# Kept inputs of a convolution: four 24-row turns become one 128-row turn

## The chip, the cores and the metric

One core of a Trainium2 chip runs one program. The metric is the device time of one execution in microseconds (us), as the median over runs. The engines are named as the profile names them: PE is TensorE (PEld its weight loads), DVE is VectorE, ACT is ScalarE, POOL is GpSimd, and SP is the engine on whose queue almost all transfers (DMAs) are issued.

## The reference, cut to what matters

Two decoder layers run over a prompt of 1024 tokens and over 8 samples of 4 tokens each. Layer 0 is sliding-window attention. Layer 1 is gated DeltaNet, and the change is in it. Its input projection gives q, k, v, z and two gates; q, k and v (4096 channels in all) pass a causal convolution of 4 taps over time, channel by channel:

```python
xqkv, z, a, b = jnp.split(h @ w_in, [GDN_CONV_CH, ...], axis=-1)
xpad = jnp.concatenate([conv_buf.astype(xqkv.dtype), xqkv], axis=1)
conv = lax.conv_general_dilated(xpad, conv_w[:, None, :], ..., feature_group_count=GDN_CONV_CH)
conv = jax.nn.silu(conv)
q, k, v = jnp.split(conv, [GDN_K_W, 2 * GDN_K_W], axis=-1)
```

For the prompt `conv_buf` is zero. For the samples it is the input `state_gdn_conv`: the 3 last inputs of each of the 8 samples, 24 rows of 4096 channels. These are the "kept inputs". A chunked delta rule over 16 value heads (8 query/key heads) follows, then a norm, a gate by z and an output projection. New conv and delta-rule states are outputs too.

## The kernel before

The activations stand transposed, with channels on the 128 partitions and the 1056 tokens (1024 of the prompt, then 32 of the samples) along the free axis. The projection of layer 1 goes in channel tiles of 128: `project` multiplies a tile's weights with all tokens in three groups of 512, 256 and 288 tokens, and each group is 24 matmuls (8 slices of the model width, times three products of high and low float32r halves: wh and wl of the weights, h2hi and h2lo of the activations) into a PSUM bank `ps_pj`. There are two such banks.

The list `SEQ` gives the order of the tiles. A head group (`hq`, 8 of them) has a k tile, a q tile and two v tiles; 16 z tiles stand between. `conv(ct, ...)` projects one of the 32 tiles that are convolved. Its `evac` copies each group from the bank to `XR` on ACT (two buffers of XR), does tap 0 on ACT, and weaves in the job `taps`, which does taps 1 to 3 on DVE and a SiLU on ACT. With the third group, which holds the samples, it fetches the tile's 24 kept rows into `st` (24 x 128, one buffer) and weaves in the job `samples`. That one turns `st` on PE (`ps_tr<-cst,st`), turns 128 columns of XR (`ps_tr<-cst,XR`), copies the kept inputs to `XS` and the new conv state to `cvo` on ACT, sends `cvo` out, and does the samples' taps on POOL.

All other work of the layer is woven between the projection's matmuls as jobs too: `decay_blocks` masks the tiles `DP` on DVE and takes their exponentials on ACT; `solve` and `invert` invert 32 x 32 blocks on DVE (`X` and `tmp`, 31 steps of two instructions per head group), send them through DRAM (`Xdd`, `Xc`) and spread them on POOL (`Xd`); `blocks` builds the inverse `UZ` on PE; `chain` runs the recurrence chunk by chunk (`vo`, `us`, `uo`, `S`); `gating` turns the result for the output projection.

The order is planned while the program is built. `Core` records each instruction and keeps a modelled time per engine; a job goes on when `ready`, `soon`, `idle` or `bank` says so by that model. `K` gives each job's rank, and `LATE` holds single steps back, by job name, how often that job has been woven, and step:

```python
if eng in self.last:
    self.tc.add_manual_dep(ins, self.last[eng], ..., reason="program order")
...
d = LATE.get((e[2], e[4], e[5]))
...
return nc.free["tensor"] < e[6] + d
```

The compute engines run in the order that was recorded. Transfers on SP are not tied to it. Since every instruction goes through one wrapper, the profile names line 90 for nearly all of them; they are told apart by the names of the tiles.

Of the kernel before, what the change touches and what calls it, by code (L numbers as in the profile page):

```python
# [5 lines left out]
F32 = mybir.dt.float32  # L6
# [8 lines left out]
P = 128  # L15
D = 1024
KD = D // P
TP = 1024
# [10 lines left out]
HQ = 8  # L29
# [197 lines left out]
def body(tc, I, O, cst_ap, dbg=None):  # L227
    nc = tc.nc
# [12 lines left out]
    turns = dict.fromkeys(rings, 0)  # L241
# [11 lines left out]
    XE = ('vector', 'vector', 'vector', 'vector', 'vector', 'scalar', 'vector', 'scalar', 'vector')  # L253
    EV = [('vector', 'scalar')] * 9
    SX = ('vector',) * 8
    K = dict(turns=4, evac=3, squares=2, scales=1, rows=0, mods=5, shapes=6, weights=7, loads=8, low=5, split=3, add=3, attend=12, turning=14, modulate=31, cached=9, wo=7, turn=0, ahead=6, taps=4, gating=5, decay=2, samples=28, load=5, mod=9, shape=9, decays=8, prepare=1, gather=11, finish=54, states=21, core=4, new=9)
    KR = [{'chain': 8, 'output': 9, 'solve': 5, 'invert': 21, 'blocks': 10, 'decayed': 0}, {'chain': 0, 'output': 3, 'solve': 12, 'invert': 10, 'blocks': 35, 'decayed': 35}, {'chain': 33, 'output': 2, 'solve': 22, 'invert': 19, 'blocks': 33, 'decayed': 34}, {'chain': 22, 'output': 12, 'solve': 3, 'invert': 4, 'blocks': 30, 'decayed': 17}, {'chain': 14, 'output': 0, 'solve': 1, 'invert': 17, 'blocks': 31, 'decayed': 57}, {'chain': 3, 'output': 13, 'solve': 6, 'invert': 20, 'blocks': 55, 'decayed': 29}, {'chain': 8, 'output': 1, 'solve': 11, 'invert': 20, 'blocks': 73, 'decayed': 34}, {'chain': 10, 'output': 8, 'solve': 4, 'invert': 28, 'blocks': 40, 'decayed': 44}]
    TB = (3, 6)
    SW = (1, 16)
# [14 lines left out]
    def psb(tag=None):  # L274
        tag = tag or any_bank
        if tag in rings:
            turns[tag] += 1
            tag = rings[tag][(turns[tag] - 1) % len(rings[tag])]
        t = ps.tile([P, 512], F32, tag=tag, name="ps_" + tag, bufs=banks[tag])
        return nc.slot(tag, banks[tag], t) if isinstance(nc, Core) else t  # L280
# [11 lines left out]
    nc = Core(tc)  # L292
# [31 lines left out]
    ident = C["ident"]  # L324
# [3 lines left out]
    rows = xp.tile([64, P], F32, name="rows")  # L328
# [190 lines left out]
    def weave(gen, name, hq=None):  # L519

        rank = KR[hq][name] if hq is not None else K[name]
        i = 0
        while i < len(jobs) and jobs[i][3] <= rank:
            i += 1
        jobs.insert(i, [lambda: True, gen, name, rank, woven.get(name, 0), 0, None])
        woven[name] = woven.get(name, 0) + 1
# [27 lines left out]
    def until(done):  # L554

        tries = 0
        while not done():
            if not stages():
                tries += 1
                assert tries < 5000, [e[1] for e in jobs]  # L560
                if not plain():
                    nc.free["tensor"] += 0.1

    def plain():
        return not isinstance(nc, Core)

    def ready(*ts):
        return lambda: plain() or nc.ready(ts) <= nc.free["tensor"]

    def soon(*ts):  # L570
        return lambda: plain() or nc.ready(ts) <= nc.free["tensor"] + AH

    def idle(eng, *ts):
        return lambda: plain() or max(nc.free[eng], nc.ready(ts)) <= nc.free["tensor"] + AI
# [7 lines left out]
    def bank(tag):  # L582

        q = held.setdefault(tag, [])
        yield lambda: len(q) < banks[tag] or q[-banks[tag]] is None
        t = psb(tag)
        q.append(t.tensor.name)
        yield lambda: plain() or nc.after(nc.used, t, "tensor") <= nc.free["tensor"]
        return t

    def give(tag, t):
        q = held[tag]
        q[q.index(t.tensor.name)] = None
# [270 lines left out]
    nc = nc.nc  # L864
# [12 lines left out]
    if True:  # L877
# [455 lines left out]
        load, step, end = modulation_gate(0, at, 8, "wg")  # L1333
# [31 lines left out]
        pt = psb()  # L1365
# [37 lines left out]
        nc = Core(tc)  # L1403
# [23 lines left out]
    if True:  # L1427
# [141 lines left out]
        for i, t in enumerate(turned_):  # L1569
# [7 lines left out]
            for kk, hf in order if i < NB else sorted(order, key=lambda o: o[::-1]):  # L1577
                if True:
                    ns = slice(hf * 512, (hf + 1) * 512)
                    if hf not in pjs:  # L1580
                        tag = ("pj", "pj", "mi", "mi")[outs[0] % 4]
# [31 lines left out]
    sconv = I["state_gdn_conv"][0].rearrange("b t c -> (b t) c")  # L1613
# [161 lines left out]
    if True:  # L1775
# [3 lines left out]
        gj = Watched(nc, gj_guard.__enter__(), since=nc.free["tensor"])  # L1779
# [3 lines left out]
        for XR in XRs:  # L1783
            nc.wide[XR.tensor.name] = GW
            nc.gpsimd.memset(XR[:, 0:3], 0.0)
            nc.gpsimd.memset(XR[:, 3 + T:], 0.0)

        def conv(ct, sm0, dst, done, run=None):

            cs = slice(ct * P, (ct + 1) * P)
            n_, XR = len(convs), XRs[len(convs) % 2]
            convs.append(0)

            def evac(gi, a0, b0, pj):
                e = min(b0, TP)
                until(lambda: (n_ < 2 or convs[n_ - 2] == 4) and open_["vT"] < VB and (gi < 2 or open_["st"] == 0))
                nc.scalar.copy(XR[:, 3 + a0:3 + b0], pj)
                u = dst(gi, a0, b0)  # L1800
                up = u[:, 0:e - a0]
                nc.scalar.activation(up, XR[:, a0:e], AF.Copy, scale=cw[:, 0, ct:ct + 1])

                def taps():
                    for i in range(1, 4):
                        yield idle("vector", up, XR[:, a0:])
                        nc.vector.scalar_tensor_tensor(up, XR[:, a0 + i:e + i], cw[:, i, ct:ct + 1], up, ALU.mult, ALU.add)
                    convs[n_] += 1
                    yield soon(up)
                    nc.scalar.activation(up, up, AF.Silu)  # L1810
                    done(gi, a0, min(b0, TP), up)

                weave(taps(), "taps")
                if gi == 2:
                    st = gj.tile([24, P], F32, tag="st", name="st")
                    nc.sync.dma_start(st, sconv[:, cs])
                    open_["st"] += 1

                    def samples():
                        yield ready(st, XR[:, TP - 64:TP], XR[:, TP:])  # L1820
                        pt = yield from bank("tr")
                        XS = gj.tile([P, DB, 7], F32, tag="XS", name="XS", bufs=2)
                        nc.tensor.transpose(pt[:, 0:24], st, ident[0:24, 0:24])
                        nc.tensor.transpose(pt[:, P:2 * P], XR[:, TP - 64:TP + 64], ident)
                        yield soon(pt)
                        nc.scalar.copy(XS[:, :, 0:3], pt[:, 0:24].rearrange("p (b t) -> p b t", t=3))
                        cvo = gj.tile([35, P], F32, tag="cvo", name="cvo")
                        nc.scalar.copy(cvo, pt[64:99, P:2 * P])
                        give("tr", pt)
                        nc.gpsimd.tensor_copy(XS[:, :, 3:7], XR[:, 3 + TP:3 + T].rearrange("p (b t) -> p b t", t=DS))  # L1830
                        nc.sync.dma_start(ncp[:, cs], cvo[0:3])
                        for t in range(1, DS):
                            nc.sync.dma_start(ncs[t - 1, :, cs], cvo[3 + t:35:DS])
                        uf = gj.tile([P, TS], F32, tag="us", name="us", bufs=2)
                        us = uf.rearrange("p (b t) -> p b t", t=DS)
                        nc.gpsimd.tensor_scalar_mul(us, XS[:, :, 0:DS], cw[:, 0, ct:ct + 1])
                        for i in range(1, 4):
                            yield idle("gpsimd")
                            tp = gj.tile([P, DB, DS], F32, tag="tp", name="tp", bufs=2)
                            nc.gpsimd.tensor_scalar_mul(tp, XS[:, :, i:i + DS], cw[:, i, ct:ct + 1])  # L1840
                            nc.gpsimd.tensor_tensor(us, us, tp, ALU.add)
                        yield soon(uf)
                        nc.scalar.activation(uf, uf, AF.Silu)
                        nc.sync.dma_start(smd[sm0], uf)
                        convs[n_] += 1
                        open_["st"] -= 1

                    weave(samples(), "samples")

            (run or projected)(evac)  # L1850

        def proj_kq(hq, st, which=(0, 1), run=None):
            for nm, ct, s0 in [(("kT", HQ + hq, HQ), ("qT", hq, 0))[w] for w in which]:
                full = gp.tile([P, T], F32, tag=nm, name=nm, bufs=2)
                st[nm] = full
                conv(ct, s0 + hq, lambda gi, a0, b0, full=full: full[:, a0:b0],
                     lambda gi, *a, nm=nm: st.update({nm + "done": gi == 2}), run)
            return st
# [411 lines left out]
        states = {0: {}}  # L2270
# [529 lines left out]
    nc = nc.nc  # L2800
# [36 lines left out]
```

## Time and profile before

| What | Value |
|---|---|
| median of 3 runs | 1669.58 us (1665.6 to 1671.26) |
| the profiled execution | 1670.08 us, its span 1668.3 us |
| busy share: PE, DVE, ACT, POOL | 95%, 73%, 52%, 34% |
| PE clock granted, mean | 0.99 |
| DMA | 191.77 MB, mean 115 GB/s |

A row of the time order reads: start in us, duration in us, engine, line, operation, output<-inputs, tile of the array, shape, count, and in brackets how long the engine stood idle before it and what ended that. Rows that follow one another with the same text are merged; their duration is that of the group. A row of waits reads: who waited, for what, us in total, times, the longest. A row by stretches of time reads: from and to, length, then busy us with the number of instructions for PE, PEld, DVE, ACT and POOL, the granted clock, the share of the DMA engines, GB/s. A row of one tile's instructions reads: shortest, median and longest duration in ns, first and last start, forms.

### The profile page before, as it was taken

The page shows a single profiled execution, that of the slowest core. Times are in us where ns is not written, and L with a number is a line of the kernel's source. Part 1 is how long each engine was busy: PE and PEld are TensorE (multiplying, and loading weights), DVE is VectorE, ACT ScalarE, POOL GpSimd, SP SyncE. Part 2 cuts the span into 40 slices and gives each one's busy share as a digit, 9 for nine tenths or more (in the row PEclk, how much of TensorE's full clock was granted, in tenths as well). Part 3 has the DMA queues.
Part 4 walks back from the last instruction along what each step waited for, and adds up shares of the span by engine and source line. Part 5 has one row for each costly group of instructions (what it writes and reads, how often), then busy time and mean ns, then how long its engine had stood idle before and what let it go on. Part 6 is the DMA issues. An engine that isn't in the chain of part 4 may idle for free. (4 is left out here: it accounts for less than half of the span.)

```text
span 1668.3 us, 31517 instructions
## 1 busy us (share of the span) xinstructions
PE 1585.5 (95%) x10594; PEld 1330.6 (80%) x10594; DVE 1210.4 (73%) x3537; ACT 869.8 (52%) x2523; POOL 568.7 (34%) x1030
## 2 busy tenths in 40 slices
PE   5999999999999989999999999999999999998996
PEld 4887877877778878889788888888888886776784
DVE  6626677564666778998888778888889876377776
ACT  6436655454445636575563664755656654342332
POOL 1201110112312325353452544445245454333431
PEclk9999999999999999999999999999999999999998
DMA  9552211224343322233322324124241238764876
GB/s 317 171 151 69 60 53 51 64 81 119 95 151 102 100 77 61 71 89 79 100 61 78 87 67 115 45 81 114 58 124 47 55 94 250 224 209 129 263 238 196
DMA packets 286036, 191.77 MB, mean 115 GB/s; under 512 B 98601, under 2 KB 260393, under 8 KB 285842
## 3 DMA queue, kind: packets, MB, share of 16 engines
q1 hardware_dynamic: 285874, 189.75, 39.7%
q8 instruction: 84, 1.38, 0.4%
q14 instruction: 78, 0.64, 0.1%
HBM read 144.68 MB, written 47.04 MB: 115 GB/s over the span
## 5 line engine op out<-in xcount | busy, mean ns | idle before, releaser
L90 PE MATMUL ps_pj<-h2hi,wh 128*128 128x512 f32 (+2 forms) x1128 | 378.8, 336 | 8.7 <-ACT XR L90 8.7
L90 PE MATMUL ps_pj<-h2hi,wl 128*128 128x512 f32 (+2 forms) x1128 | 378.8, 336 | 0.0
L90 PE MATMUL ps_pj<-h2lo,wh 128*128 128x512 f32 (+2 forms) x1128 | 377.7, 335 | 0.0
L90 POOL TENSOR_TENSOR wl<-wr,wh 128x512 fp32r<-128x512 f32 x128 | 172.1, 1345 | 569.4 <-ACT wh L90 516.9
L90 PEld LDWEIGHTS ps_pj<-h2hi,wh 128*128 128x128 f32 x1128 | 214.2, 190 | 22.6 <-ACT XR L90 9.1
L90 PEld LDWEIGHTS ps_pj<-h2lo,wh 128*128 128x128 f32 x1128 | 214.6, 190 | 14.3
L90 PEld LDWEIGHTS ps_pj<-h2hi,wl 128*128 128x128 f32 x1128 | 214.3, 190 | 14.5
L90 POOL TENSOR_TENSOR xt<-xt,y 128x512 f32<-128x512 f32 (+1 forms) x48 | 65.4, 1369 | 181.6 <-DVE y L90 118.7
L90 PE MATMUL ps_pj<-hhi,wh 128*128 128x256 f32 (+2 forms) x376 | 123.1, 331 | 2.7 <-DVE kll L90 1.5
L90 PE MATMUL ps_pj<-hlo,wh 128*128 128x256 f32 (+2 forms) x376 | 123.7, 332 | 0.0
L90 PE MATMUL ps_pj<-hhi,wl 128*128 128x256 f32 (+2 forms) x376 | 122.6, 330 | 0.0
L90 DVE SCALAR_TENSOR_TENSOR vT<-XR,cT,vT 128x256 f32<-128x256 f32 (+1 forms) x144 | 89.2, 640 | 17.1 <-ACT vT L90 15.6
L90 DVE TENSOR_TENSOR tmp<-X 64x31 f32<-64x31 f32 (+15 forms) x248 | 93.4, 376 | 8.9 <-POOL X L90 5.5
L90 DVE TENSOR_TENSOR X<-X,tmp 64x31 f32<-64x31 f32 (+15 forms) x248 | 91.6, 369 | 8.5
L90 ACT CAST wh<-wr 128x512 fp32r<-128x512 f32 x128 | 78.4, 615 | 21.9 <-PE ps_pj L90 14.5
L90 PEld LDWEIGHTS ps_pj<-hlo,wh 128*128 128x128 f32 x376 | 70.4, 188 | 14.8 <-issue 10.8
L90 PEld LDWEIGHTS ps_pj<-hhi,wh 128*128 128x128 f32 x376 | 70.4, 189 | 11.6 <-issue 6.1
L90 PEld LDWEIGHTS ps_pj<-hhi,wl 128*128 128x128 f32 x376 | 70.3, 188 | 8.2 <-issue 4.4
L90 ACT ACTIVATE vo<-vo,fo 128x128 f32<-128x128 f32 x128 | 43.2, 393 | 61.3 <-POOL fo L90 61.3
L90 ACT ACTIVATE prob<-prob,nm 128x256 f32<-128x256 f32 (+1 forms) x128 | 62.3, 489 | 18.6 <-DVE nm L90 18.3
L90 POOL TENSOR_TENSOR Xd<-Xc,cst 32x128 f32<-32x128 f32 x128 | 62.9, 491 | 18.7 <-DMA Xc<-Xdd 11.3
L90 ACT ACTIVATE qe<-ps_mi,Eg 128x128 f32<-128x128 f32 x112 | 35.0, 364 | 64.1 <-PE ps_mi L90 63.8
(558 smaller groups left out, 4091.3 us busy)
## 6 DMA issues: line engine op xcount, KB each, us to landing
wr<-in_gdn_w_in SPq DMA_DIRECT2D x96, 256.0 KB
wm<-in_w_mod SPq DMA_DIRECT2D x64, 256.0 KB
S<-in_state_gdn_s SPq DMA_DIRECT2D x38, 256.0 KB
xt<-in_x_prompt SPq DMA_DIRECT2D x16, 512.0 KB
wr<-in_swa_w_in SPq DMA_DIRECT2D x64, 128.0 KB
wmod<-in_w_mod SPq DMA_DIRECT2D x32, 256.0 KB
DP<-gcr SPq DMA_DIRECT2D x64, 128.0 KB
zl<-zd SPq DMA_DIRECT2D x32, 256.0 KB
```

The source lines that it names most:

```text
L90: inst = fn(*args, **kwargs)
```

## The change

The kept rows of one head group's four tiles (k, q and the two v) are fetched together, at the group's k tile, into one tile of 128 partitions: tile q at rows 32q to 32q+23, the rest zero. A job `kept` turns all four at once on PE and copies the result from PSUM to `so` on ACT. The job `samples` then takes its 24 columns from `so`, and turns only XR. Both tiles have two buffers, cleared once on POOL. The number of loads stays 32; the PE turns of kept rows go from 32 of 24 rows to 8 of 128 rows; 8 copies on ACT are new.

```diff
-    K = dict(... taps=4, gating=5, decay=2, samples=28, load=5, ...)
+    K = dict(... taps=4, gating=5, decay=2, samples=28, kept=7, load=5, ...)
...
+        rows4, old4, kept_, passed = [], [], {}, [0] * HQ
+        for i in range(2):
+            rows4.append(gj.tile([P, P], F32, name=f"st{i}"))
+            old4.append(gj.tile([P, P], F32, name=f"so{i}"))
+            nc.gpsimd.memset(rows4[i], 0.0)
+
+        def keep(hq):
+
+            st, so = rows4[hq % 2], old4[hq % 2]
+            for q, ct in enumerate((HQ + hq, hq, 2 * HQ + 2 * hq, 2 * HQ + 2 * hq + 1)):
+                nc.sync.dma_start(st[32 * q:32 * q + 24], sconv[:, ct * P:(ct + 1) * P])
+
+            def turn():
+                yield ready(st)
+                yield lambda: hq < 2 or passed[hq - 2] == 4
+                pt = yield from bank("tr")
+                nc.tensor.transpose(pt[:, 0:P], st, ident)
+                yield soon(pt)
+                nc.scalar.copy(so, pt[:, 0:P])
+                give("tr", pt)
+                kept_[hq] = so
+
+            weave(turn(), "kept")
...
+            hq, q4 = (ct, 1) if ct < HQ else (ct - HQ, 0) if ct < 2 * HQ else (ct // 2 - HQ, 2 + ct % 2)
+            if q4 == 0:
+                keep(hq)
             convs.append(0)
...
                 if gi == 2:
-                    st = gj.tile([24, P], F32, tag="st", name="st")
-                    nc.sync.dma_start(st, sconv[:, cs])
                     open_["st"] += 1
 
                     def samples():
-                        yield ready(st, XR[:, TP - 64:TP], XR[:, TP:])
+                        yield lambda: hq in kept_ and ready(XR[:, TP - 64:TP], XR[:, TP:])()
                         pt = yield from bank("tr")
                         XS = gj.tile([P, DB, 7], F32, tag="XS", name="XS", bufs=2)
-                        nc.tensor.transpose(pt[:, 0:24], st, ident[0:24, 0:24])
-                        nc.tensor.transpose(pt[:, P:2 * P], XR[:, TP - 64:TP + 64], ident)
+                        nc.tensor.transpose(pt[:, 0:P], XR[:, TP - 64:TP + 64], ident)
                         yield soon(pt)
-                        nc.scalar.copy(XS[:, :, 0:3], pt[:, 0:24].rearrange("p (b t) -> p b t", t=3))
+                        nc.scalar.copy(XS[:, :, 0:3], kept_[hq][:, 32 * q4:32 * q4 + 24].rearrange("p (b t) -> p b t", t=3))
                         cvo = gj.tile([35, P], F32, tag="cvo", name="cvo")
-                        nc.scalar.copy(cvo, pt[64:99, P:2 * P])
+                        nc.scalar.copy(cvo, pt[64:99, 0:P])
                         give("tr", pt)
...
                         convs[n_] += 1
+                        passed[hq] += 1
                         open_["st"] -= 1
```

Since the plan follows from modelled times, the edit moves other instructions on every engine too. Three places matter below.

PE, in the projection at the second group's k tile (XR_6048 is that tile's buffer), before:

```order
L90 MATMUL ps_pj<-h2hi,wl 128x512
L90 MATMUL ps_pj<-h2hi,wh 128x512
L90 MATMUL ps_tr<-cst,st 128x24
L90 MATMUL ps_tr<-cst,XR_6048 128x128
L90 MATMUL ps_pj<-h2lo,wh 128x512
```

and now:

```order
L90 MATMUL ps_pj<-h2lo,wh 128x512
L90 MATMUL ps_pj<-h2hi,wl 128x512
L90 MATMUL ps_tr<-cst,XR_6048 128x128
L90 MATMUL ps_pj<-h2hi,wh 128x512
L90 MATMUL ps_pj<-h2lo,wh 128x512
```

The turn of st is gone from here; the group's one turn of 128 rows stands earlier, in the k tile's own group of 256 tokens.

ACT, at the second head group: the SiLUs of its k tile (kT<-kT), the exponentials of DP, and the copies that empty the projection's banks for the first v tile (XR_6049<-ps_pj), before:

```order
L90 ACTIVATE kT<-kT 128x512
L90 COPY XS<-ps_tr 128x8x3
L90 COPY cvo<-ps_tr 35x128
L90 CAST wh<-wr 128x512
L90 ACTIVATE kT<-kT 128x256
L90 ACT_TABLE_LOAD
L90 ACTIVATE DP<-DP 128x512 x4
L90 COPY XR_6049<-ps_pj 128x512
L90 ACTIVATE vT<-XR_6049,cT 128x512
L90 ACT_TABLE_LOAD
L90 ACTIVATE us<-us 128x32
L90 ACTIVATE kT<-kT 128x256
```

and now:

```order
L90 ACTIVATE kT<-kT 128x512
L90 CAST wh<-wr 128x512
L90 COPY XR_6049<-ps_pj 128x512
L90 ACTIVATE vT<-XR_6049,cT 128x512
L90 ACT_TABLE_LOAD
L90 ACTIVATE DP<-DP 128x512 x4
L90 ACT_TABLE_LOAD
L90 ACTIVATE us<-us 128x32
L90 ACTIVATE kT<-kT 128x256
L90 COPY XR_6049<-ps_pj 128x256
L90 ACTIVATE vT<-XR_6049,cT 128x256
L90 ACTIVATE kT<-kT 128x256
```

The copy of the group of 512 moved ahead of the exponentials and of a SiLU; the copy of the group of 256 still follows them.

PE, at the end of the projection (the last matmul of a tile, `ps_pj<-h2hi,wl 128x288`) and before the output projection (`ps_pj<-h2hi,ohi`); UZ and M are the last head group's blocks, before:

```order
L90 MATMUL ps_pj<-h2hi,wl 128x288
L90 MATMUL ps_lg<-UZ,M 32x96 x2
L90 MATMUL ps_lg<-UZ,M 32x64 x2
...
L90 MATMUL ps_ob<-vo,UZ 128x128 x2
L90 MATMUL ps_lg<-UZ,M 32x96 x8
L90 MATMUL ps_mi<-us,ktok 128x256
L90 MATMUL ps_mi<-uo,DP 128x128 x2
L90 MATMUL ps_mi<-S,kT 128x256
L90 MATMUL ps_lg<-modG,selt 128x512 x2
L90 MATMUL ps_ob<-vo,UZ 128x128 x2
L90 MATMUL ps_pj<-h2hi,ohi 128x512
```

and now:

```order
L90 MATMUL ps_pj<-h2hi,wl 128x288
L90 MATMUL ps_mi<-uo,DP 128x128 x2
L90 MATMUL ps_mi<-S,kT 128x256
L90 MATMUL ps_ob<-vo,UZ 128x128 x2
L90 MATMUL ps_mi<-us,ktok 128x256
L90 MATMUL ps_lg<-modG,selt 128x512 x2
L90 MATMUL ps_mi<-S,qT 128x256
L90 MATMUL ps_mi<-uo,DP 128x128 x2
L90 MATMUL ps_mi<-S,kT 128x256
L90 MATMUL ps_ob<-vo,UZ 128x128 x2
L90 MATMUL ps_pj<-h2hi,ohi 128x512
```

The blocks moved ahead of the end of the projection, and one more chunk of the last chain stands between the two projections.

More of the change, by code (lines that the diff above doesn't have):

```diff
@@ L255, in body @@
     SX = ('vector',) * 8
-    K = dict(turns=4, evac=3, squares=2, scales=1, rows=0, mods=5, shapes=6, weights=7, loads=8, low=5, split=3, add=3, attend=12, turning=14, modulate=31, cached=9, wo=7, turn=0, ahead=6, taps=4, gating=5, decay=2, samples=28, load=5, mod=9, shape=9, decays=8, prepare=1, gather=11, finish=54, states=21, core=4, new=9)
+    K = dict(turns=4, evac=3, squares=2, scales=1, rows=0, mods=5, shapes=6, weights=7, loads=8, low=5, split=3, add=3, attend=12, turning=14, modulate=31, cached=9, wo=7, turn=0, ahead=6, taps=4, gating=5, decay=2, samples=28, kept=7, load=5, mod=9, shape=9, decays=8, prepare=1, gather=11, finish=54, states=21, core=4, new=9)
     KR = [{'chain': 8, 'output': 9, 'solve': 5, 'invert': 21, 'blocks': 10, 'decayed': 0}, {'chain': 0, 'output': 3, 'solve': 12, 'invert': 10, 'blocks': 35, 'decayed': 35}, {'chain': 33, 'output': 2, 'solve': 22, 'invert': 19, 'blocks': 33, 'decayed': 34}, {'chain': 22, 'output': 12, 'solve': 3, 'invert': 4, 'blocks': 30, 'decayed': 17}, {'chain': 14, 'output': 0, 'solve': 1, 'invert': 17, 'blocks': 31, 'decayed': 57}, {'chain': 3, 'output': 13, 'solve': 6, 'invert': 20, 'blocks': 55, 'decayed': 29}, {'chain': 8, 'output': 1, 'solve': 11, 'invert': 20, 'blocks': 73, 'decayed': 34}, {'chain': 10, 'output': 8, 'solve': 4, 'invert': 28, 'blocks': 40, 'decayed': 44}]
```

## The prediction

> **What bounds the kernel now.** I read the page's busy times first, then the busy time of each engine over the three parts of the program, then what TensorE (PE) waited for between 520 and 1400 us, the stage to which all changed lines belong.
>
> ```profile
> PE 1585.5 (95%) x10594; PEld 1330.6 (80%) x10594; DVE 1210.4 (73%) x3537; ACT 869.8 (52%) x2523; POOL 568.7 (34%) x1030
> ...
> 520.00:1400.00 880.00, 848.21 (x6042) 748.83 (x6041) 717.65 (x1994) 512.39 (x1559) 386.99 (x846) 0.99 0.32 85
> ...
> PE ps_pj L90 <- ACT XR L90: 8.7, 2, 7.7
> ```
>
> The reader is to see that PE is the bound: 848.2 of 880 us in this stage. So an instruction taken out of PE's stream is worth its place in that stream, nearly in full, and the other 31.8 us are waits, which the order of the work decides. One wait of 7.7 us is a quarter of them.
>
> **What a turn costs.** The 32 turns of 24 rows each stand directly ahead of the turn of XR:
>
> ```profile
> L90 SPq DMA_DIRECT2D st<-in_state_gdn_conv x32: 313/336/1303, 525.4 to 1335.5; - x32
> L90 PE MATMUL ps_tr<-cst,st x32: 236/236/238, 551.8 to 1356.8; 24*128 24x24 f32 x32
> ...
> 702.62 0.39 PE L90 MATMUL ps_pj<-h2hi,wl 128*128 128x512 f32 x1
> 702.85 0.40 PE L90 MATMUL ps_pj<-h2hi,wh 128*128 128x512 f32 x1
> 703.18 0.24 PE L90 MATMUL ps_tr<-cst,st 24*128 24x24 f32 x1
> 703.35 0.33 PE L90 MATMUL ps_tr<-cst,XR 128*128 128x128 f32 x1
> 703.43 0.48 PE L90 MATMUL ps_pj<-h2lo,wh 128*128 128x512 f32 x1
> 703.75 0.40 PE L90 MATMUL ps_pj<-h2hi,wl 128*128 128x512 f32 x1
> ...
> 637.51 0.39 PE L90 MATMUL ps_pj<-h2hi,wh 128*128 128x512 f32 x1
> 637.74 0.40 PE L90 MATMUL ps_pj<-h2lo,wh 128*128 128x512 f32 x1
> 637.98 0.38 PE L90 MATMUL ps_tr<-cst,vT 128*128 128x128 f32 x2
> 638.12 0.48 PE L90 MATMUL ps_pj<-h2hi,wl 128*128 128x512 f32 x1
> 638.43 0.28 PE L90 MATMUL ps_pj<-h2hi,wh 128*128 128x256 f32 x1
> ...
> 609.62 0.19 PEld L90 LDWEIGHTS ps_pj<-h2hi,wh 128*128 128x128 f32 x1
> 610.18 0.13 PEld L90 LDWEIGHTS ps_tr<-cst,st 24*128 24x128 f32 x1 [0.37 <-issue]
> ```
>
> Durations of matmuls overlap, so the price is read from starts. The projection's matmuls of 512 columns start every 0.23 us (702.62 to 702.85). From 702.85 to 703.75 are two of those steps and the pair of turns: 0.90 - 0.46 = 0.44 us for the pair. Two turns of full 128 rows in the same stream (637.74 to 638.43): 0.69 - 0.46 = 0.23, or 0.11 each. So the XR turn alone should cost 0.11 and the 24-row turn 0.33, three times a full one. The last two rows say why: weights of the usual tiles are loaded while the matmul ahead still runs, but the load of the 24-row tile stood idle for 0.37 us with nothing named as its releaser and began together with its own matmul.
>
> The Trainium skill, TensorEngine Tiling (Array Packing), section "Tiling Modes", says that changing the tiling mode, not only the tile, drains TensorE; that is what the idle weight load looks like, and a tile padded to 128 rows stays in the mode of its neighbours.
>
> **The sum, against the profiled execution's 1670.08 us** (span 1668.3 and 1.8 around it; the median of the three runs is 1669.58, so the sum stands 0.5 us above the median's scale, which I do not correct).
>
> 1. Turns on PE. Out: 32 x 0.33 = 10.6 us. In: 8 full turns x 0.11 = 0.9 us. Net -9.7. The other end is to count only the 0.17 from the start of st to that of XR: then 32 x 0.17 = 5.4 out, 8 x (0.44 - 0.17) = 2.2 in, net -3.2. I take -9.7, because the two full turns are the nearest thing to what remains. Three of the 32 stand where PE waits anyway: the one at 610.18 ahead of the long wait, and these two, where a later or earlier operand on ACT ends the wait:
>
> ```profile
> 725.66 0.24 PE L90 MATMUL ps_tr<-cst,st 24*128 24x24 f32 x1 [0.64 <-ACT vo L90]
> ...
> 1334.60 0.33 PE L90 MATMUL ps_tr<-cst,XR 128*128 128x128 f32 x1 [0.47 <-ACT XR L90]
> ```
>
> That returns 3 x 0.33 = 1.0: **-8.7**.
>
> 2. The long wait. The order of all engines is planned while the program is built, and the edit moves it. At this wait ScalarE (ACT) had to empty the projection's bank, behind other work:
>
> ```profile
> 617.81 0.28 PE L90 MATMUL ps_pj<-h2hi,wl 128*128 128x256 f32 x1
> 625.78 0.61 PE L90 MATMUL ps_pj<-h2hi,wh 128*128 128x288 f32 x1 [7.69 <-ACT XR L90]
> ...
> 616.60 0.64 ACT L90 ACTIVATE kT<-kT 128x512 f32<-128x512 f32 x1 [6.31 <-DVE kT L90]
> 617.50 0.62 ACT L90 CAST wh<-wr 128x512 fp32r<-128x512 f32 x1
> 621.22 0.42 ACT L90 ACTIVATE kT<-kT 128x256 f32<-128x256 f32 x1 [3.10 <-DVE kT L90]
> 621.64 1.28 ACT L90 ACT_TABLE_LOAD   x1
> 622.93 2.19 ACT L90 ACTIVATE DP<-DP 128x512 f32<-128x512 f32 x4
> 625.14 0.59 ACT L90 COPY XR<-ps_pj 128x512 f32<-128x512 f32 x1
> ...
> 621.77 0.64 DVE L90 SCALAR_TENSOR_TENSOR DP<-DP,gc,cst 128x128 f32<-128x128 f32 x2
> ...
> 625.00:630.00 5.00, 4.22 (x18) 4.21 (x19) 4.74 (x12) 4.33 (x10) 0.00 (x0) 0.52 0.04 7
> ```
>
> ACT is in order: the copy of XR stood behind a SiLU that waited for VectorE (DVE), a table load and four exponentials, though its bank was full at about 615. The new order puts this copy ahead of them, behind the SiLU of 512 and a cast: about 616.9 + 0.5 + 0.6 = 618.0, so the wait at 617.9 goes. But the copy of the next 256 columns is still behind the exponentials, and those behind all 16 masks of DP on DVE. The last mask was done at 622.4; in the new order one more tap of kT (about 0.5) and one more X step of two instructions (0.9) precede it: 623.8. The last exponential takes 0.6, the table load 1.28, two SiLUs 0.6, the copy 0.4: 626.7. PE has one group of 288 columns (24 x 0.13 = 3.2 us) to do meanwhile, and then waits from 621.3 to 626.8, 5.5 us where it was 7.7. That is late next. The half clock after the wait (0.52 in the row) is paid again. Gain 7.7 - 5.5 = 2.2; I take **-2.5**, between -5 (the masks come no later) and +5 (DVE falls further behind).
>
> 3. The end of the stage. The last head's blocks now stand ahead of the last projection matmuls, not behind them:
>
> ```profile
> 1383.96 0.29 PE L90 MATMUL ps_pj<-h2hi,wl 128*128 128x288 f32 x1
> ...
> 1391.16 1.22 PE L90 MATMUL ps_mi<-uo,DP 128*128 128x128 f32 x4 [2.49 <-ACT uo L90]
> ...
> 1397.78 0.49 PE L90 MATMUL ps_pj<-h2hi,ohi 128*128 128x512 f32 x1
> ...
> 1369.35 7.83 POOL L90 TENSOR_TENSOR Xd<-Xc,cst 32x128 f32<-32x128 f32 x15 [0.47 <-DMA Xc<-Xdd]
> ```
>
> These 13.8 us without projection work shrink by up to 5: the blocks' copies, and the 2.49 us. But the blocks follow from Xc, which landed at 1369.35 and comes perhaps 1 to 2 us earlier by DVE's new order; PE would then wait for Xd earlier instead. **-1.5**, between -5 and +2.
>
> 4. All other waits are dealt anew. The least and the most busy 100 us of the stage, without those that hold the long wait and the stage's end:
>
> ```profile
> 900.00:1000.00 100.00, 94.71 (x678) 81.69 (x678) 78.27 (x224) 60.53 (x196) 46.85 (x108) 1.00 0.30 78
> ...
> 1200.00:1300.00 100.00, 99.87 (x721) 88.63 (x719) 86.61 (x244) 61.52 (x195) 44.99 (x103) 1.00 0.33 88
> ```
>
> PE's idle time goes from 0.1 to 5.3 us per 100. The delays in the table LATE go by job name, number and step and stay, while their neighbours change. I put **+4**, a little less than one stretch turned from the best to the worst, with 7 either way (half that spread, 2.6, in each of eight stretches, added as independent).
>
> 5. The start. Four loads of kept rows now go out at once, ahead of weights, and PE turns them near 526. The nearest row is the load of wab, issued at 519.62 and awaited on ACT until 523.47:
>
> ```profile
> 519.62 1.01 SPq L90 DMA_DIRECT2D wab<-in_gdn_w_in  x2
> ...
> 523.47 0.30 ACT L90 CAST wab<-wab 128x128 fp32r<-128x128 f32 x1 [0.56 <-DMA wab<-in_gdn_w_in]
> ...
> 529.48 0.58 ACT L90 COPY abT<-ps_lg 64x512 f32<-64x512 f32 x1 [3.55 <-PE ps_lg L90]
> ```
>
> 3.9 us from issue to use: issued from about 521.7, four at 0.34, the rows are there near 526 to 527. **+1**, from 0 to 3.
>
> At nothing: the loads stay 32 of the same size on SP.
>
> ```profile
> SPq L90 <- PE ps_tr L90: 115.2, 30, 13.0
> ```
>
> Nearly each used to wait there for the turn before it (one buffer), and weight loads with it; now it waits for the turn two heads back. PE's waits name no weight load, so what SP gains is not on the path: the spare weight buffers hide it, and would hide as much again if a group of four loads stood first (4 x 0.34 = 1.3 us). ACT gets 8 copies of 128x128, each shorter than the 0.59 of the 512-column copy above, while it is busy 512 of 880 us; and two more table loads (1.28 each) near the start, where it sat idle for 3.55 us ahead of abT; if that cover goes, 2.6 us are late. POOL clears two more tiles at the stage's start, and is busy for a third of the span.
>
> Sum: -8.7 - 2.5 - 1.5 + 4 + 1 = -7.7; 1670.1 - 7.7 = **1662.4 us**.
>
> **The rivals.** (a) The narrow turn is cheap, and the rest of the 0.44 belongs to the XR turn (a change of bank, a semaphore), which stays. For it: st to XR is only 0.17. Against it: the idle weight load stands at st, not at XR, and the full turns change banks too without it. Priced by columns, 24 against 128, a narrow turn is 0.02 and PE gains nothing (0.7 out, 0.9 in): 1670.1 + 0.2 + 1.0 for items 2 to 5 = 1671.3; with 0.17 it is 1670.1 - 3.2 + 1.0 = 1667.9. No change.
>
> The Trainium skill states that pricing in TensorE: Matmul & The Clock Gate, section "Part 2: What happens when you issue a matmul": back to back, a matmul costs as many cycles as it has columns. The trace agrees for equal tiles (128 columns 0.11, 512 columns 0.23 with another type) and not for the 24-row tile.
>
> (b) Slower: the long wait is met twice. Exponentials of DP stand once per head in ACT's queue; at the fourth head the new order puts an XR copy directly behind them, as at the long wait before. If DVE's masks are as late there, that is 7.7 us and some 1.4 at low clock more. With items 2 and 3 gaining nothing: 1670.1 - 8.7 + 4 + 1 + 9.1 = 1675.5. It decides once the masks end more than 3 us (a group on PE) after the bank is full. Against it: before, a copy behind exponentials cost that once in eight heads.
>
> (c) More gain: items 2 and 3 at their low ends and no loss in 4 and 5: 1670.1 - 8.7 - 10 = 1651.4.
>
> **Chances.** 0.3% is 5 us, about what a measurement of this kernel can tell from no change: bounds 1664.6 and 1674.6. Forecast 0.52 (of it 0.06 above 1664.6), (a) 0.24, (b) 0.16, (c) 0.08. So faster 0.54, same 0.30, slower 0.16. The forecast's own range is 1656 to 1667; to hold eight in ten, with (a) and the near parts of (b) and (c), 1652 to 1674.
>
> **What would show it.** Right: no matmul of 24 rows; XR turns that add about 0.11 to the projection's steps and no idle weight load before them; PE busy some 9 us less between 520 and the first output matmul; the wait at 618 gone and one of 5 to 6 us one group later; idle PE elsewhere about as before. Wrong: XR turns alone that still start 0.33 after the matmul ahead (then (a)); a wait of PE for ACT XR over 6 us at another head (then (b)); PE waiting for its first turn of st.

## The result and the profile after

The changed kernel takes 1695.66 us (median of 4 runs, 1691.43 to 1698.86), the kernel before 1670.18 us (median of 4, 1665.6 to 1671.26): ratio 1.0163, 95% interval 1.0147 to 1.018. By the medians it is 25.5 us slower, where 7.7 us of gain were forecast. The profiled execution is one of 1694.69 us; its span is 1692.8 us, 24.5 more than before.

The page's busy times after; then the stretch from 520 us to the first matmul of the output projection, and the rest, before and after:

```profile
PE 1588.5 (94%) x10570; PEld 1332.4 (79%) x10570; DVE 1209.8 (71%) x3537; ACT 874.1 (52%) x2533; POOL 572.7 (34%) x1032
```

```profile
520.00:1397.78 877.78, 845.99 (x6033) 746.97 (x6031) 716.14 (x1988) 510.89 (x1556) 386.82 (x845) 0.99 0.31 84
1397.78:1668.30 270.52, 243.35 (x1200) 185.24 (x1199) 181.58 (x525) 95.98 (x236) 89.91 (x107) 0.97 0.71 215
...
520.00:1412.53 892.53, 844.74 (x6025) 748.27 (x6025) 720.34 (x1990) 518.07 (x1574) 392.19 (x848) 0.99 0.31 83
1412.53:1692.80 280.27, 247.15 (x1185) 185.82 (x1184) 177.92 (x525) 94.08 (x231) 88.61 (x107) 0.95 0.68 206
```

PE has 24 instructions less and is 3.0 us longer busy; it is idle for 1692.8 - 1588.5 = 104.3 us, where it was 82.8. So the 24.5 us are 21.5 us of waiting and 3.0 us of work, though work was taken out. They aren't one wait. From the timeline of PE, behind 505 us, the waits of over 1 us are 26 with 48.4 us in all, where they were 12 with 28.0. Six of the new ones, among them the first and the longest:

```profile
560.89 0.33 PE L90 MATMUL ps_tr<-cst,XR 128*128 128x128 f32 x1 [1.53 <-ACT XR L90]
...
949.10 0.50 PE L90 MATMUL ps_pj<-h2hi,wl 128*128 128x512 f32 x1 [1.69 <-POOL wl L90]
...
1365.48 0.66 PE L90 MATMUL ps_tr<-cst,vT 128*128 128x128 f32 x4 [2.39 <-ACT vT L90]
...
1406.23 1.22 PE L90 MATMUL ps_mi<-us,ktok 128*128 128x256 f32 x2 [3.11 <-DVE us L90]
...
1428.67 0.63 PE L90 MATMUL ps_lg<-S,zq 128*32 128x256 f32 x4 [2.96 <-DMA S<-in_state_gdn_s]
...
1519.69 0.80 PE L90 MATMUL ps_ob<-h2hi,ohi 128*128 128x512 f32 x1 [4.30 <-DVE y L90]
```

Their releasers are ACT, POOL, DVE and a transfer, with no one tile in common. The last projection matmul and the first one of the output projection, after:

```profile
1400.51 0.29 PE L90 MATMUL ps_pj<-h2hi,wl 128*128 128x288 f32 x1
...
1412.53 0.47 PE L90 MATMUL ps_pj<-h2hi,ohi 128*128 128x512 f32 x1
```

The projections end 16.6 us later than before (1383.96), and from the first output matmul to the end are 280.3 us, where there were 270.5. So 9.8 of the 24.5 us lie in a stage of which the change touches no instruction; the new plan puts that stage in another order too, and its granted clock is 0.95 where it was 0.97.

### The profile page after: what moved, and what is told of

Same layout as the page of the kernel before. It is cut to its first block, busy times and chain, and to the rows that moved or that the text cites. A ratio compares the mean times of both kernels' runs of the same rounds, so it can differ in the third digit from the quotient of the medians.

```text
span 1692.8 us, 31442 instructions
## 1 busy us (share of the span) xinstructions
PE 1588.5 (94%) x10570; PEld 1332.4 (79%) x10570; DVE 1209.8 (71%) x3537; ACT 874.1 (52%) x2533; POOL 572.7 (34%) x1032
## 5 line engine op out<-in xcount | busy, mean ns | idle before, releaser
L90 POOL TENSOR_TENSOR wl<-wr,wh 128x512 fp32r<-128x512 f32 x128 | 176.5, 1381 | 566.5 <-ACT wh L90 512.7
L90 DVE TENSOR_TENSOR X<-X,tmp 64x31 f32<-64x31 f32 (+15 forms) x248 | 97.0, 391 | 8.5
L90 PEld LDWEIGHTS ps_pj<-hhi,wh 128*128 128x128 f32 x376 | 70.5, 189 | 11.5 <-issue 6.1
L90 ACT COPY XR<-ps_pj 128x512 f32<-128x512 f32 (+2 forms) x96 | 43.2, 450 | 58.8 <-PE ps_pj L90 58.5
```

The costliest lines, as they stand in the source:

```text
L90: inst = fn(*args, **kwargs)
```

## The experiments

Two theories. **A, the order:** the change as such saves time, and the plan, which is made anew, deals every other instruction into an order that is worse. **B, what the change adds:** eight more users of the one bank for turns, eight copies on ACT and loads in fours hold PE up. To part them, some kernels below hide a change from the planner: the class that records the order is told that the old instruction was issued, while another one is put in its place. The order of all the rest is then that of the kernel before, instruction for instruction on PE, ACT, DVE and POOL. Behind a ratio, gains and losses in us are the ratio's, times 1670 us.

### The change in the order of before

```diff
+ def unseen(self, eng, op, *args, model=None):     # issued in recorded order; the planner sees only model
...
- nc.tensor.transpose(pt[:, 0:24], st, ident[0:24, 0:24])
+ if passed[hq] == 0:
+     nc.unseen("tensor", "transpose", pt[:, 0:P], rows4[hq % 2], ident)
+ nc.issued("tensor", "transpose", None, (pt[:, 0:24], st, ident[0:24, 0:24]), {})
...
- nc.scalar.copy(XS[:, :, 0:3], pt[:, 0:24]...)
+ if passed[hq] == 0:
+     nc.unseen("scalar", "copy", old4[hq % 2], pt[:, 0:P])
+ nc.unseen("scalar", "copy", XS[:, :, 0:3], old4[hq % 2][:, 32 * q4:32 * q4 + 24]..., model=(XS..., pt[:, 0:24]...))
```

> The whole change (four kept loads into one tile, eight turns of 128 rows, eight more copies on ACT), but with the plan made as if it were not there: every other instruction of PE, ACT, DVE and POOL stands in the order of the kernel before. Theory A (the order): the change as such saves PE time, and the loss of 25 us comes from the new order of everything else. It expects a gain between the turns' price by starts (6.5 us: 5.4 behind the narrow turns and 1.4 behind XR's turns, less 0.3 for eight full ones) and the forecast's 9.7, so 1660.5 to 1663.7. Theory B (what the change adds): eight more users of the single PSUM bank of the turns, eight copies on ACT and loads in fours hold PE up more than the narrow turns did. It expects about the time of the changed kernel, 1685 or more.

Measured: 1663.87 us (7 runs), ratio to before 0.9972 (0.996 to 0.9983), that is 4.7 us faster (2.8 to 6.7), as theory A has it to within 0.2 us. The same loads, turns and copies take some 32 us less here than in the changed kernel, so they are not what B needs. One part of B this kernel leaves out: its full turn shares a visit to the bank with XR's turn, as the narrow one did, while the changed kernel takes that bank eight times more. The changed kernel's own trace speaks for these visits. In the whole of it PE waits once for a copy of `so`:

```profile
819.98 0.33 PE L90 MATMUL ps_tr<-cst,vo 128*128 128x128 f32 x1 [2.26 <-ACT so L90]
```

At the same turn the kernel before waited 2.55 us for another result of ACT (`vo`). ACT itself stands idle for 7.1 us in all ahead of three of the eight copies, and behind none of those three turns does PE wait within 5 us. So theory B falls here as well, though by what PE waits for and not by a run of its own. The page's busy times, and in PE's timeline XR's turn where no kept turn stands with it:

```profile
PE 1578.8 (95%) x10570; PEld 1330.8 (80%) x10570; DVE 1210.6 (73%) x3537; ACT 871.6 (52%) x2531; POOL 576.3 (35%) x1032
```

```profile
758.84 0.39 PE L90 MATMUL ps_pj<-h2hi,wl 128*128 128x512 f32 x1
759.06 0.39 PE L90 MATMUL ps_pj<-h2hi,wh 128*128 128x512 f32 x1
759.29 0.27 PE L90 MATMUL ps_tr<-cst,XR 128*128 128x128 f32 x1
759.32 0.48 PE L90 MATMUL ps_pj<-h2lo,wh 128*128 128x512 f32 x1
759.64 0.39 PE L90 MATMUL ps_pj<-h2hi,wl 128*128 128x512 f32 x1
```

From 759.06 to 759.64 are two steps of 0.23 and 0.12 for XR's turn, where the pair took 0.44. So 0.32 is the price of a narrow turn (0.33 was forecast), and 32 x 0.32 - 8 x 0.12 = 9.3 us left the stream at their places. PE's busy time fell by 6.7 us, its idle time rose by 0.5 (1662.1 - 1578.8 = 83.3), and 4.7 us reached the end.

### Full turns for narrow ones

```diff
- nc.tensor.transpose(pt[:, 0:24], st, ident[0:24, 0:24])
+ nc.unseen("tensor", "transpose", pt[:, 0:P], rows4[n_ % 2], ident, model=(pt[:, 0:24], st, ident[0:24, 0:24]))
```

> The kernel before, order and loads kept, but each 24-row tile of kept inputs padded with zeros to 128 rows, so that the 32 turns stay 32 and are full ones. It asks what makes the narrow turn dear. If it is the change of shape on PE (forecast: 0.33 us against 0.11 for a full one), 32 x 0.22 = 7.0 us are saved: 1663.2. If a turn costs by its columns (rival a of the prediction: 24 columns 0.02, 128 columns 0.11), 32 x 0.09 = 2.9 us are lost: 1673.1. If only the 0.17 from its start to the next are its own, 32 x 0.06 = 1.9 us are saved: 1668.3.

Measured: 1664.6 us (8 runs), ratio 0.9979 (0.9962 to 0.9996), 3.5 us faster (0.7 to 6.3). Turns of 128 columns in the place of turns of 24 columns are not slower, so columns are not the price. In PE's timeline (instructions put in past the planner have the line of that helper, L165):

```profile
701.40 0.39 PE L90 MATMUL ps_pj<-h2hi,wh 128*128 128x512 f32 x1
701.63 0.27 PE L165 MATMUL ps_tr<-cst,st 128*128 128x128 f32 x1
701.74 0.27 PE L90 MATMUL ps_tr<-cst,XR 128*128 128x128 f32 x1
701.77 0.48 PE L90 MATMUL ps_pj<-h2lo,wh 128*128 128x512 f32 x1
702.08 0.39 PE L90 MATMUL ps_pj<-h2hi,wl 128*128 128x512 f32 x1
```

The pair takes 0.68 - 0.46 = 0.22, as two full vT turns did (0.23), where it took 0.44: 32 x 0.22 = 7.0 us in place, of which the 3.5 reached the end. The interval takes in the 1.9 us of the third expectation; the rows decide for the first.

### The narrow turn twice

```diff
  nc.tensor.transpose(pt[:, 0:24], st, ident[0:24, 0:24])
+ nc.unseen("tensor", "transpose", pt[:, 2 * P:2 * P + 24], st, ident[0:24, 0:24])     # the first kernel: in a row
  nc.tensor.transpose(pt[:, P:2 * P], XR[:, TP - 64:TP + 64], ident)
+ nc.unseen("tensor", "transpose", pt[:, 2 * P:2 * P + 24], st, ident[0:24, 0:24])     # the second: behind XR's turn
```

> The kernel before in its own order, with each of the 32 narrow turns issued twice in a row (the second one's result is read by nothing). If the price is that of changing PE's shape, the second one finds it set and costs what its 24 columns take, at most 0.06 us: 0.6 to 2 us more, 1669.5 to 1671, and the step from the first to the second is far under 0.17. If every narrow turn costs by itself what taking it out has saved (5.4 + 1.6 us over 32, 0.22 each), 7.0 us more: 1676.

> The same, with the second narrow turn behind the turn of XR, so that PE's shape changes once more. If the price is that of the change of shape, it is paid in full again: 32 x 0.22 = 7.0 us (what taking one out has saved) to 32 x 0.33 = 10.6 us (the forecast): 1676 to 1680. If the first turn is dear only because it waits for something else at its place (its weights, the bank), the second is cheap wherever it stands: 1669 to 1671.

Measured: twice in a row 1669.99 us (12 runs), ratio 1.0009 (0.9995 to 1.0022); apart 1674.11 us (7 runs), ratio 1.0043 (1.0025 to 1.006), 7.2 us slower. The stream of PE, twice in a row:

```profile
633.46 0.40 PE L90 MATMUL ps_pj<-h2hi,wh 128*128 128x512 f32 x1
633.78 0.24 PE L90 MATMUL ps_tr<-cst,st 24*128 24x24 f32 x1
633.87 0.21 PE L165 MATMUL ps_tr<-cst,st 24*128 24x24 f32 x1
634.01 0.33 PE L90 MATMUL ps_tr<-cst,XR 128*128 128x128 f32 x1
634.10 0.47 PE L90 MATMUL ps_pj<-h2lo,wh 128*128 128x512 f32 x1
634.41 0.39 PE L90 MATMUL ps_pj<-h2hi,wl 128*128 128x512 f32 x1
```

and apart:

```profile
609.15 0.40 PE L90 MATMUL ps_pj<-h2hi,wh 128*128 128x512 f32 x1
609.48 0.24 PE L90 MATMUL ps_tr<-cst,st 24*128 24x24 f32 x1
609.65 0.33 PE L90 MATMUL ps_tr<-cst,XR 128*128 128x128 f32 x1
609.91 0.24 PE L165 MATMUL ps_tr<-cst,st 24*128 24x24 f32 x1
610.07 0.50 PE L90 MATMUL ps_pj<-h2lo,wh 128*128 128x512 f32 x1
610.41 0.39 PE L90 MATMUL ps_pj<-h2hi,wl 128*128 128x512 f32 x1
```

In a row the turns take 0.95 - 0.46 = 0.49, 0.05 more than one narrow turn and XR's; apart they take 1.26 - 0.46 = 0.80, 0.36 more. A second narrow turn costs 0.05 where the shape is set and 0.36 where it changes: the price is that of the change of shape. (The second turn in a row has the same weights, but they were loaded again, for 0.14 us at 633.84; so a saved load is not what makes it cheap.) This agrees with the Trainium skill, TensorEngine Tiling (Array Packing), section "Tiling Modes", by which a change of the tiling mode drains TensorE; the 0.36 us is this kernel's number. Here too less reaches the end than stands in the stream: 32 x 0.36 = 11.5 us in place, 7.2 at the end.

### The new order with the narrow turns put back

```diff
+ nc.unseen("tensor", "transpose", pt[:, P:P + 24], st, ident[0:24, 0:24])
  nc.tensor.transpose(pt[:, 0:P], XR[:, TP - 64:TP + 64], ident)
...
- nc.scalar.copy(XS[:, :, 0:3], kept_[hq][:, 32 * q4:32 * q4 + 24]...)
+ nc.unseen("scalar", "copy", XS[:, :, 0:3], pt[:, P:P + 24]..., model=(XS..., kept_[hq]...))
```

> The changed kernel, its order kept, with the 32 loads and turns of 24 rows put back in front of XR's turns (unknown to the plan); the eight full turns and copies stay, and nothing reads them. Theory A: the new order loses more than the changed kernel shows, since the turns' saving hides part of it; with the narrow turns back it is 6.5 to 9.7 us slower than the changed kernel's 1695.7, so 1702 to 1705. If a narrow turn costs next to nothing, it stays at 1695 to 1697.

Measured: 1699.47 us (5 runs), ratio to before 1.0178 (1.0161 to 1.0195). Against the changed kernel's 1.0163 that is 2.5 us more, and the intervals overlap: it cannot be told from nothing, and the time lies between the two expectations. It does show that the new order with all 32 narrow turns in it (and the eight full ones beside them) is 30 us slower than the kernel before.

### Other orders of the same instructions

```diff
+ nc.free["tensor"] += 0.3        # the plan alone: PE is taken to be 0.3 us later (second kernel: 1.0)
  XRs, convs = [gj.tile([P, TP + 64], F32, name=f"XR{i}") for i in range(2)], []
```

> The kernel before with the same instructions, and a plan that starts this stage with PE 0.3 us later than before: nothing is added or taken out, but the order moves about as much as by the change (1662 differing rows of 8009 on PE, against 1642 for the change). Theory A: the order of before is an unusually good one, for which the table LATE and the ranks were set, so another order of the same instructions loses some 15 to 40 us (the change's 25.5 us and the 6.5 to 9.7 us that its turns saved make 32 to 35): 1685 to 1710. Theory B: orders are worth about the same, 1665 to 1675.

> A second order of the same instructions as before: the plan starts the stage with PE 1.0 us later (1344 differing rows on PE, and as different from the first re-planned order as that is from before's). If the order of before is an unusually good one, this loses too, by the 15.7 us of the first re-planned order give or take 10: 1675 to 1695. If the first one was bad by chance, this one is as likely below 1669 as above.

The table LATE, which holds jobs back by name, number and step, emptied in both kernels:

```diff
- LATE = {('ahead', 57, 2): 0.8, ...
+ LATE = {}
```

> The kernel before with the table LATE emptied: the same instructions, planned without its 37 hand-set delays. Theory A1 (the table is what makes the order of before good, and what misfires in any other): the loss is of the size of the re-planned orders seen so far, 15 to 35 us, 1684 to 1704. Theory A2 (the table matters little, the fit lies in the ranks): less than 8 us, 1667 to 1678.

> The changed kernel with the table LATE emptied. A1: without the table neither order has been fitted, and the change is worth what it was worth in an order held still, some 5 us: 1679 to 1699, below the kernel before without its table, and no slower than the changed kernel with it (1695.7). A2: the table does in the changed kernel what it does before, so emptying it costs the same few us: 1696 to 1704.

Measured, each against the runs of before beside it; span, PE busy and PE idle (their difference) are those of the profiled executions:

| kernel | us | ratio (95%) | span | PE busy | PE idle | clock |
|---|---|---|---|---|---|---|
| before | 1670.18 | 1 | 1668.3 | 1585.5 | 82.8 | 0.990 |
| change, order of before | 1663.87 | 0.9972 (0.996 to 0.9983) | 1662.1 | 1578.8 | 83.3 | 0.989 |
| the change | 1695.66 | 1.0163 (1.0147 to 1.018) | 1692.8 | 1588.5 | 104.3 | 0.986 |
| before, plan 0.3 us later | 1684.61 | 1.0097 (1.0082 to 1.0112) | 1686.4 | 1595.6 | 90.8 | 0.983 |
| before, plan 1.0 us later | 1687.84 | 1.0113 (1.0096 to 1.013) | 1686.5 | 1590.3 | 96.2 | 0.985 |
| before, no LATE | 1702.39 | 1.0201 (1.0185 to 1.0216) | 1702.8 | 1600.0 | 102.8 | 0.981 |
| the change, no LATE | 1687.81 | 1.0113 (1.0098 to 1.0128) | 1685.4 | 1591.4 | 94.0 | 0.983 |

Two nudges of the plan that add and remove nothing cost 16 and 19 us. So the order of before is not one of many like it: each of the five new orders in the table lies 16 to 33 us above it. What the table LATE has to do with that is less clear. Without it the kernel before loses 33 us and the changed kernel gains 8 (1695.66 to 1687.81), as if its delays fitted the old neighbours and did harm among the new ones. But emptying it makes one more new order of each kernel, and the orders here differ by more than 8 us among themselves, so the gain may not be the table's doing. With both orders unfitted the changed kernel is 14.6 us the faster; that is one pair of orders, and no measure of the change. The 37 delays were not tried one by one. In each of these orders PE's busy time is higher too, and its clock lower, than in the order of before: between the changed kernel and the same instructions in the old order, 9.7 us of busy time. The clock accounts for some 5 of them by estimate (1588.5 x 0.003 / 0.989, from 0.986 against 0.989). More changes of PE's shape are not the rest: from the first projection matmul to the first output matmul both traces have 73 (the kernel before has 137). Where the rest lies is open.

### The change in another order

The same edit as in the first experiment, with the plan 0.3 us later.

> The change laid into the first re-planned order (the one that starts the stage 0.3 us later), held still as in the run that laid it into the order of before. If the change is worth the same whatever the order, 5.0 us (2.8 to 6.7) less than that order without it (1684.6): 1677.9 to 1681.8. If its worth depends on which waits the order has, anything from 1675 to 1690.

Measured: 1683.05 us (4 runs), ratio 1.0082 (1.0056 to 1.0108); that order without the change has 1.0097. The gain, 2.5 us, lies below the expected range and is less than the two intervals can tell from none or from 5, so whether the change is worth the same in another order is undecided.

### The long wait taken apart

With the change in the order of before, PE's long wait and ACT ahead of it, the second fence from ACT's timeline:

```profile
622.07 0.61 PE L90 MATMUL ps_pj<-h2hi,wh 128*128 128x288 f32 x1 [5.21 <-ACT XR L90]
```

```profile
617.50 0.42 ACT L90 ACTIVATE kT<-kT 128x256 f32<-128x256 f32 x1 [1.71 <-DVE kT L90]
617.93 1.28 ACT L90 ACT_TABLE_LOAD   x1
619.22 2.19 ACT L90 ACTIVATE DP<-DP 128x512 f32<-128x512 f32 x4
621.43 0.59 ACT L90 COPY XR<-ps_pj 128x512 f32<-128x512 f32 x1
```

```diff
- for dt_ in DP: nc.scalar.activation(dt_, dt_, AF.Exp)
+ for dt_ in DP: nc.issued("scalar", "activation", None, (dt_, dt_), {})      # second head group alone: the plan is told the old place
...
  nc.scalar.activation(up, XR[:, a0:e], AF.Copy, scale=...)
+ for dt_ in DP: nc.unseen("scalar", "activation", dt_, dt_, AF.Exp)          # behind the second XR copy, or the first
```

> The change in the order of before, and one thing more: at the long wait of PE for ACT's copy of XR (5.2 us at 622 with the change in that order) the table load and the four exponentials of DP are put behind ACT's next two copies of XR; no other instruction changes place, since the plan isn't told. If the wait is made by what stands ahead of the copy on ACT, it falls by the 1.28 + 2.19 = 3.5 us that stand there, and some half of a us at low clock goes with it: 1663.9 - 3.5 to 4 = 1660. If the exponentials, now some 3 us later, hold up work that uses DP, that is given back and it stays near 1663.9.

Measured: 1669.17 us (12 runs), ratio 0.9995 (0.9982 to 1.0007): nearly all of the change's 4.7 us is lost again, more than either expectation had it. PE's waits there, then ACT:

```profile
620.81 0.40 PE L90 MATMUL ps_pj<-h2hi,wh 128*128 128x288 f32 x1 [1.73 <-ACT XR L90]
625.89 0.44 PE L90 MATMUL ps_lg<-cst,kT 128*128 128x128 f32 x2 [0.97 <-ACT kT L90]
633.12 0.47 PE L90 MATMUL ps_tr<-cst,XR 128*128 128x128 f32 x1 [5.10 <-ACT XR L90]
```

```profile
625.29 0.23 ACT L90 ACTIVATE us<-us 128x32 f32<-128x32 f32 x1 [3.78 <-POOL us L90]
...
625.74 0.35 ACT L90 COPY XR<-ps_pj 128x256 f32<-128x256 f32 x1
```

The first wait fell by the 3.5 us. But the exponentials had stood over a wait of ACT for POOL's us; without them ACT stands idle there for 3.78 us and runs them later, and PE waits 5.10 us for the copy of XR behind them.

> As the run before, but the table load and the four exponentials go behind one copy of XR (and the first tap behind it), not two; everything after them stays where it was. In the run before, the copies behind the second place waited 3.78 us for POOL's us and the wait came back as 5.1 us at the turn of XR. Here the first wait should fall by some 3.5 us; the next copies keep their times, so that PE, which then comes to the next bank 3.5 us earlier, waits there up to 2 us; net 1.5 to 3.5 us less than the change in the order of before (1663.9): 1660.4 to 1662.4. If instead the wait comes back in full, as in the run before, 1664 to 1669.

Measured: 1664.0 us (11 runs), ratio 0.9971 (0.9962 to 0.998), the same as without the move, as the second expectation had it. PE's waits:

```profile
622.36 0.40 PE L90 MATMUL ps_pj<-h2hi,wh 128*128 128x288 f32 x1 [2.68 <-ACT XR L90]
628.48 0.44 PE L90 MATMUL ps_lg<-cst,kT 128*128 128x128 f32 x2 [2.00 <-ACT kT L90]
632.21 0.33 PE L90 MATMUL ps_tr<-cst,XR 128*128 128x128 f32 x1 [1.58 <-ACT XR L90]
```

5.21 us have become 2.68 + 2.00 + 1.58 = 6.26. A wait of PE that is only the first of several behind the same engines isn't worth its length.

The fastest version found is the change in the order of before, 0.9972 of the kernel before.

## Why the prediction was wrong, point by point

1. **Turns on PE (-8.7).** The mechanism and the price in the stream were right: 0.32 per narrow turn, 0.12 per full one, and the change of shape as its cause, not columns (rival a falls). That equal tiles go by columns is seen in the projection's own steps (512, 288 and 256 columns: 0.23, 0.13 and 0.11 us); the two figures set side by side under rival (a), of different types, do not show it. Mis-sized is what reaches the end: 4.7 us (2.8 to 6.7) of 9.3, and in the two other kernels 3.5 of 7.0 and 7.2 of 11.5. The premise was that an instruction taken out is worth its place "nearly in full", and I took off 1.0 for three turns inside waits; in fact about half did not arrive, on a PE that is 95% busy. Why is open. Waits that grow where PE comes earlier are one reason (PE's idle time fell from 82.8 to 74.9 where the narrow turns stand twice and apart, 1670.3 - 1595.4), but with the change in the order of before idle time rose by 0.5 only, and it is the busy time that fell by 6.7 and not by 9.3.
2. **The long wait (-2.5).** Right in its steps, some 2.5 us later than forecast. After:

```profile
619.60 0.60 ACT L90 CAST wh<-wr 128x512 fp32r<-128x512 f32 x1
620.23 0.59 ACT L90 COPY XR<-ps_pj 128x512 f32<-128x512 f32 x1
...
621.59 1.28 ACT L90 ACT_TABLE_LOAD   x1
622.88 1.15 ACT L90 ACTIVATE DP<-DP 128x512 f32<-128x512 f32 x2
624.43 0.63 ACT L90 ACTIVATE DP<-DP 128x512 f32<-128x512 f32 x1 [0.39 <-DVE DP L90]
626.70 0.63 ACT L90 ACTIVATE DP<-DP 128x512 f32<-128x512 f32 x1 [1.64 <-DVE DP L90]
...
629.08 0.35 ACT L90 COPY XR<-ps_pj 128x256 f32<-128x256 f32 x1
```

```profile
622.44 0.29 PE L90 MATMUL ps_pj<-h2hi,wh 128*128 128x288 f32 x1
...
629.48 0.50 PE L90 MATMUL ps_pj<-h2hi,wh 128*128 128x512 f32 x1 [3.71 <-ACT XR L90]
```

   The copy of 512 is ahead of the exponentials, the group of 288 starts without a wait, and one group later PE waits behind exponentials that wait for DVE's masks: 3.71 us, where 5.5 were forecast and 7.69 stood before. (With the order of before, the wait is 5.21 with the change and 6.27 to 7.29 in the three kernels with other turns.) That this wait fell from 7.69 and the kernel still lost 25 us is the clearest sign that a single wait was the wrong thing to look at.
3. **The end of the stage (-1.5).** From the last projection matmul to the first output matmul it is 12.0 us, where it was 13.8: -1.8. The number is right by luck. The same stretch takes 12.5 us with the change in the order of before, where the blocks have not moved, and the wait of 2.49 us that was to shrink is replaced by one of 3.11 (the row at 1406.23). PE is idle in it for 4.0 us after and 3.9 before.
4. **All other waits (+4, with 7 either way).** This is the step that failed. The span grew by 24.5 us although items 1 to 3 took off some 8 to 10.5 (4.7 for item 1 as measured in the old order, 4.0 and 1.8 for the others; 2.5 of the 4.0 may stand in the 4.7 too). That leaves, by estimate, some +33 to +35 for items 4 and 5, where +5 was put. Between the profiled executions of the same instructions in the two orders it is 30.7 us (1692.8 - 1662.1): 21.0 of waiting and 9.7 of busy time. So two of the signs named ahead failed: PE is 1.3 us less busy up to the first output matmul (845.99 to 844.74) and not some 9, and idle PE elsewhere is not as before. The size came from the spread between stretches of one and the same order, an order that the ranks and the table had been fitted to. Its spread says how well it fits here and there; it says nothing of orders that nobody fitted. The orders measured that nobody had fitted lie 16 to 33 us above before. What in the new order makes PE wait more, beyond the rows above, stays open: no one wait holds it. I also counted only the stage that holds the changed lines, and 9.8 us came in the output stage.
5. **The start (+1).** PE waited for no turn of st. The projection still stood 4.7 us behind by 575 us (570.17 before, 574.86 after, for the same group), with 0.8 of it from before the projection (its first matmul is at 518.75 and 519.58) and 1.53 in the first row of new waits above: the rest of it belongs to item 4.

Rival (b), the long wait met twice, did not come about: no wait for ACT's XR above 3.71. The sign came out on its side for another reason, so that is luck.

## What to carry to other kernels

Where a plan orders the instructions, an edit is two changes, the instructions and the order; measure the first with the order held still, by telling the planner the old story, before believing either sign. A plan tuned by tables keyed to its jobs is a fitted thing: an edit that it sees can cost what the fit was worth (here 16 to 33 us, against 5 for the change), and nudging the plan with nothing changed shows how much that is. A turn of few rows between full ones was worth padding to full rows here: it cost its change of shape, not its columns.

## What the runs showed of the hardware that was not expected

On this kernel's PE, 95% busy, work put into its stream or taken out of it passed to the end at some half to two thirds (9.3 us to 4.7, 7.0 to 3.5, 11.5 to 7.2; each has an interval of some 2 to 3 us either way, so the shares are rough). And the change of shape of PE's tile is paid once per visit here: 0.36 us for a lone narrow turn between full ones, 0.05 for a second one next to it.
